# Two-layer decoder trunk: transposes of the norm dealt over two banks by pairs of blocks, bias table in 32 copies, no adaLN steps in the value part

## The chip, the cores and the metric

One NeuronCore of a Trainium2 chip runs the whole kernel as one program. The metric is device microseconds of one execution. The chip shares its work among TensorE (PE: matmuls and transposes; its weight loads are PEld), VectorE (DVE), ScalarE (ACT), GpSimd (POOL), SyncE (SP, which here only issues DMAs) and 16 DMA engines.

## What is computed

```python
for l in range(2):                                   # x is 256 x 1024, float32
    mod = silu(c) @ w_ada[l] + b_ada[l]              # adaLN: 9 vectors of 1024
    h = pre(x, 0); x += 0.5 * mod[0, 2] * (silu(h @ wg) * (h @ wu)) @ wd        # FFN, d_ff 2816
    h = pre(x, 1)                                    # pre: rmsnorm(x) * gain * (1 + scale) + shift
    q, k, v, ..., gates = split(h @ w_in[l])         # 4 stick-breaking, 6 dilated, 6 sliding-window heads
    x += mod[1, 2] * (sum_b sigmoid(g_b) * (o_b @ w_br_b)) @ w_out
    h = pre(x, 2); x += 0.5 * mod[2, 2] * (silu(h @ wg2) * (h @ wu2)) @ wd2     # second FFN
return rmsnorm(x)
```

The dilated and sliding-window heads add a bias to their scores: for each head a row of 383 values by distance (-1e30 where a key is masked), of which query row p takes the 256 values from 127 - p on.

## The kernel before

**Numbers.** Every weight and every activation is split in two fp32r parts, a high part H (a cast) and a low part L (the remainder), and each product is three matmuls: H by H, H by L, L by H. All weights, 280 MB, are read from HBM once.

**Units.** The weights come as 1 MB pieces (`raw`, three buffers) on SP's DMA queue, and each piece is cut in two units of 128 x 1024. `feed` (line 147) keeps five units ahead of PE: ACT casts a unit's high part (`wH`, line 144), DVE subtracts to get the low part (`wL`, line 160), and when a piece's last unit is subtracted, `load_raws` issues the load of the next piece. PE waits for a unit only when these run late. All instructions are issued in an order that is written out by hand; each engine and each queue runs its own list in order.

**Six sub-layers** (s = 0 to 5: FFN, mixer, FFN, FFN, mixer, FFN). The adaLN vectors of later sub-layers are computed in between: `ada_tick`, called once for every unit, adds to a credit by the table `PACE` (line 48; one tuple for each sub-layer, one number for each of its parts, scaled so that the steps due are done in time) and runs `ada_step` for each whole credit: a 512 KB load on SP's queue and a multiply-add of 128 x 1024 on DVE (L284; the first of each eight on ACT, L282). For the mixers (s = 1 and 4) the parts are: the six units of the value part, the 14 of q and k, the three gated branches (10, 10 and 12), and the output.

**The change of sub-layers** (`run_rows`, line 765). The 256 tokens are two halves, t = 0 and 1. While PE ends the last matmuls of half 1, the norm of half 0 runs: `norm_x` scales x (`xn`), `norm_pe` (line 484) has PE transpose its eight blocks of 128 features into two PSUM banks (`psn`), blocks 0 to 3 in the first and 4 to 7 in the second, and `norm_evac` (line 495) applies scale and shift on the way out: DVE takes the first bank (L508), ACT the second (L510), four blocks each, into `h32`. `norm_high` (line 520, L523) casts one half of the features on ACT to the high part of the new `hHL`, `norm_low` (line 525, L529) subtracts on DVE. Between the casts ACT still squares the last quarter of x for half 1 (`jk`, line 455). Then PE runs `early()`: the first two units of the next sub-layer for half 0 (`ffn_early` line 852, `v_early` line 1009), which read these features; for an FFN both units read blocks 0 to 3, for a mixer unit 0 reads blocks 0 to 3 and unit 1 blocks 4 to 7. After them comes the same for half 1, where the high part is written straight from PSUM.

**Bias table.** In the first FFN `bias_table` (line 426) adds the mask on DVE (`mk`, 12 heads x 383) and writes it eight times over to a DRAM tile `scr` with eight DMAs on POOL's queue (L433). At the start of each mixer `load_bias` (line 435) loads the 128 x 12 x 256 table `Tm` with 16 DMAs on POOL's queue (L442), each for eight neighbouring partitions; partition r + i takes its rows from copy i, shifted by one value. The table is first used in the dilated branch, some 75 us later.

**Stick-breaking heads.** Among the q and k units of a mixer run, for two pairs of heads (`sb_stages`, placed by line 1245): scores `pz`, exponentials on ACT (`e`, L1045), sums by PE (`pc`, L1057), a subtraction on DVE (`z`, L1060), the exponential of it on ACT (L1064), and PE's product with v (`po`, L1073).

Of the kernel before, what the change touches and what calls it, by code (L numbers as in the profile page):

```python
# [10 lines left out]
F32 = mybir.dt.float32  # L11
# [5 lines left out]
P = 128  # L17
# [3 lines left out]
KB = D // P  # L21
FF = 2816
NF = FF // P
NHEAD = 12
NDIST = 383
# [19 lines left out]
N1 = (0, 0, 1, 1, 0, 0)  # L45

START_PACE = 0.3
PACE = ((1, 0.75, 1, 1.25), (1, 1, 1, 1, 0.75, 0.75), (1, 1, 1, 1), (1, 1, 1, 0.75), (1, 2, 0, 0, 1, 2),
        (1, 1, 1, 1))
SPARE = (5, 1, 1, 1, 1, 1)  # L50
SOON = 5
# [38 lines left out]
class Trunk:  # L90
# [335 lines left out]
    def bias_table(self):  # L426
        nc, oh, mk, rb = self.nc, self.oh, self.mk, self.rb
        p = self.ps("psr")
        nc.tensor.matmul(p[:NHEAD, :NDIST], rb, oh, start=True, stop=True)
        nc.vector.tensor_tensor(mk, p[:NHEAD, :NDIST], mk, op=ALU.add)  # L430
        self.scr = self.dp.tile([NHEAD, 8, NDIST], F32, tag="scr", name="scr")
        for r in range(8):
            nc.gpsimd.dma_start(self.scr[:, r, :], mk)  # L433

    def load_bias(self, T):


        for r in range(0, P, 8):
            base = self.scr[:, 0:8, 0:256]
            src = bass.AP(tensor=base.tensor, offset=base.offset + P - 1 - r,  # L440
                          ap=[[NDIST - 1, 8], [8 * NDIST, NHEAD], [1, 256]])
            self.nc.gpsimd.dma_start(T[r:r + 8], src)  # L442


    def square(self, t, cols, tag):
# [37 lines left out]

    def norm_pe(self, t, s, xn):

        ps = []
        for q in range(2):
            p = self.ps(f"psn{s}_{t}_{q}")
            for i in range(4):
                fb = 4 * q + i  # L490
                self.nc.tensor.transpose(p[:, i * P:(i + 1) * P], xn[:, fb * P:(fb + 1) * P], self.ident)
            ps.append(p)
        return ps

    def norm_evac(self, t, s, ps, between=()):

        nc = self.nc
        h32 = self.work([P, KB, P], f"h32_{s}_{t}")
        sl = slice(t * P, (t + 1) * P)

        def evac(out):
            for i in range(4):
                for q in range(2):
                    fb = 4 * q + i
                    sa, sb = self.modv[:, s, 1, fb:fb + 1], self.modv[:, s, 0, fb:fb + 1]
                    src = ps[q][:, i * P:(i + 1) * P]
                    if q == 0:
                        nc.vector.tensor_scalar(out[:, fb, :], src, sa, sb, ALU.mult, ALU.add)  # L508
                    else:
                        nc.scalar.activation(out[:, fb, :], src, AF.Identity, bias=sb, scale=sa)  # L510

        if t == 1:
            evac(self.hH[:, :, sl])
            for f in between:
                f()
            self.feed(2)
        evac(h32)
        return h32

    def norm_high(self, t, h32, q):  # L520
# [244 lines left out]
    def run_rows(self, us, s, xh, xl, early=None):  # L765
# [54 lines left out]
        piece(1, end, tail[LEAD:])  # L820
        self.done(TAIL)
        h0 = self.norm_evac(0, s + 1, p0)
        self.norm_high(0, h0, 0)
        self.mean_eps(1)
        self.residual(1, end, s, pd[1, end])
        self.norm_high(0, h0, 1)
# [1 line left out]
        left = [(ch[1], self.ada_reduce(ch)) for ch in nxt[:n1]]  # L828
# [5 lines left out]
        p1 = self.norm_pe(1, s + 1, xn1)  # L834
        left += [(ch[1], self.ada_reduce(ch)) for ch in nxt[n1:]]
        for kind, fs in left:
            if kind < 2:
                fs[0]()
        h1 = self.norm_evac(1, s + 1, p1, [fs[1] for kind, fs in left if kind < 2])
        self.norm_low(1, h1)  # L840
        self.feed()
        for kind, fs in left:
            if kind == 2:
# [7 lines left out]

    def ffn_early(self, plan):

        for u in plan["in"][:2]:
            u.pe(u, (0,))

    def run_ffn(self, plan, early=None):
        s = plan["s"]
# [150 lines left out]
    def v_early(self, plan):  # L1009

        s = plan["s"]
        plan["pv"] = [[self.ps(f"pv{s}_{t}_{i}") for i in range(2)] for t in range(2)]
        for i, part in enumerate(("all", "high")):
            self.v_pe(i, plan["v"][i], plan["pv"], (0,), part)

    def v_post(self, t, pv):
# [252 lines left out]
    def run(self):  # L1269
# [100 lines left out]
        for n, plan in enumerate(plans):  # L1370
# [7 lines left out]
            else:  # L1378
                k = len(plan["in"])
                parts = [k // 4, k // 4, k - k // 4 * 2, NF - TAIL]  # L1380
            self.pace = sum(([w] * k for w, k in zip(PACE[s], parts)), [])
            f = need / sum(self.pace)
# [42 lines left out]
```

## Time and profile before

| | |
|---|---|
| three executions | 1200.52, 1202.75, 1202.95 us; median 1202.75 |
| the profiled execution | 1201.48 us, its span 1199.7 us, mean granted clock 0.995 |
| PE (matmul) busy | 1172.9 us, 98% of the span, 7105 instructions |
| weight loads, DVE, ACT, POOL busy | 1023.3, 830.7, 607.4, 37.8 us |
| DMA | 285.15 MB, 238 GB/s in the mean; SP's queue 279.88 MB, POOL's queue 3.93 MB |
| chain that ended last | PE 84%, DMA 5%, DVE 4%, ACT 4% |

PE is nearly always busy, so a change is worth what it takes from PE's idle time, of which there are 27 us in all, or from the time in which PE runs at a lower clock. The start of the program and its end hold most of the idle time; the rest is a few waits of about 1 us.

### The profile page before, as it was taken

Reading aid. Unit: us, or ns where it says so; the run is one execution under the profiler, and the core shown is the slowest. Engines: PE = TensorE matmul, PEld = TensorE weight load, DVE = VectorE, ACT = ScalarE, POOL = GpSimd, SP = SyncE. Lnnn points to the kernel's source line nnn. Section 1 sums busy time; section 2 is a strip of 40 time slices with the busy share of each in tenths; the row PEclk is TensorE's granted clock in tenths of the full one; section 3 lists DMA queues with packets and bytes.
Section 4 is the critical chain, followed back from the end, with each engine's and each line's share of the span. In section 5 each row is a group of like instructions: output and inputs, shape, how many; then the busy total and the mean of one; then the engine's idle time right before and its main releaser. Section 6 shows DMA issues by size and latency. Waiting matters only on the chain.

```text
span 1199.7 us, 17743 instructions
## 1 busy us (share of the span) xinstructions
PE 1172.9 (98%) x7105; PEld 1023.3 (85%) x7105; DVE 830.7 (69%) x1011; ACT 607.4 (51%) x877; POOL 37.8 (3%) x74
## 2 busy tenths in 40 slices
PE   6999999999999999999999999999999999999997
PEld 6988888989999878888878888889999997888886
DVE  3677777667788787677677676665866787555544
ACT  5554443565564465444365444355655446544432
POOL 1001000300000000000000000011000000000000
PEclk9999999999999999999999999999999999999999
DMA  9988889796568668888839877759863573665550
GB/s 319 310 317 308 282 300 332 120 339 210 195 200 308 228 231 295 282 299 277 287 121 335 280 252 270 251 162 210 283 208 110 185 268 139 223 196 182 182 176 36
DMA packets 151516, 285.15 MB, mean 238 GB/s; under 512 B 8006, under 2 KB 78956, under 8 KB 151432
## 3 DMA queue, kind: packets, MB, share of 16 engines
q1 hardware_dynamic: 148744, 279.88, 68.9%
q0 software_dynamic: 2544, 3.93, 2.5%
q8 instruction: 56, 0.92, 0.3%
q14 instruction: 28, 0.23, 0.1%
q10 hardware_dynamic: 144, 0.20, 0.0%
HBM read 282.77 MB, written 1.20 MB: 237 GB/s over the span
## 4 chain that ended last, share of the span: by engine, by line
PE 84%; DMA 5%; DVE 4%; ACT 4%; issue 2%; POOL 1%; SPq 0%; POOLq 0%; ACTq 0%; DVEq 0%
PE pf L672 35%; PE pd L763 21%; PE pg L603 12%; PE pq L603 4%; PE pb L603 3%; DMA raw<-in_w_in 2%; PE pf L633 2%; PE pft L698 2%; DVE wL L160 1%; DMA ada<-in_w_ada 1%; PE adag L345 1%; ACT wH L144 1%; ACT jk L455 1%; DVE acc L284 1%; ACT h L510 1%
## 5 line engine op out<-in xcount | busy, mean ns | idle before, releaser
L160 DVE TENSOR_TENSOR wL<-raw,wH 128x1024 fp32r<-128x1024 f32 (+1 forms) x384 | 462.2, 1212 | 264.5 <-ACT wH L144 262.2
L144 ACT CAST wH<-raw 128x1024 fp32r<-128x1024 f32 (+1 forms) x384 | 395.8, 1045 | 386.7 <-PE pf L672 155.1
L672 PE MATMUL pf<-wH,hHL 128*128 128x512 f32 (+1 forms) x1408 | 418.5, 378 | 3.4 <-ACT hHL L523 3.4
L672 PEld LDWEIGHTS pf<-wH,hHL 128*128 128x128 f32 x1408 | 258.6, 188 | 53.8 <-ACT hHL L523 4.3
L672 PE MATMUL pf<-wL,hHL 128*128 128x512 f32 (+1 forms) x704 | 260.9, 375 | 0.0
L672 PEld LDWEIGHTS pf<-wL,hHL 128*128 128x128 f32 x704 | 132.6, 188 | 23.7 <-issue 0.7
L284 DVE SCALAR_TENSOR_TENSOR acc<-ada,sc,acc 128x1024 f32<-128x1024 f32 x112 | 143.3, 1279 | 3.9 <-DMA ada<-in_w_ada 3.9
L603 PE MATMUL pg<-hHL,wH 128*128 128x256 f32 x768 | 145.4, 285 | 0.0
L763 PE MATMUL pd<-wH,ffH 128*128 128x512 f32 x336 | 131.6, 392 | 0.0
L763 PE MATMUL pd<-wH,ffL 128*128 128x512 f32 x336 | 130.8, 389 | 0.0
L763 PE MATMUL pd<-wL,ffH 128*128 128x512 f32 x336 | 130.8, 389 | 0.0
L603 PEld LDWEIGHTS pg<-hHL,wH 128*128 128x128 f32 x768 | 121.8, 192 | 2.7 <-issue 0.9
L603 PE MATMUL pg<-hHL,wL 128*128 128x256 f32 x384 | 94.0, 283 | 0.0
L603 PE MATMUL pq<-hHL,wH 128*128 128x256 f32 x448 | 85.4, 289 | 1.0 <-ACT wH L144 1.0
L763 PEld LDWEIGHTS pd<-wH,ffH 128*128 128x128 f32 x336 | 63.1, 188 | 13.6 <-issue 0.8
L763 PEld LDWEIGHTS pd<-wH,ffL 128*128 128x128 f32 x336 | 63.1, 188 | 13.3
L763 PEld LDWEIGHTS pd<-wL,ffH 128*128 128x128 f32 x336 | 63.1, 188 | 12.8
L603 PEld LDWEIGHTS pq<-hHL,wH 128*128 128x128 f32 x448 | 71.8, 195 | 2.0 <-ACT wH L144 1.2
L603 PEld LDWEIGHTS pg<-hHL,wL 128*128 128x128 f32 x384 | 73.4, 191 | 0.0
L603 PE MATMUL pq<-hHL,wL 128*128 128x256 f32 x224 | 56.1, 287 | 1.8 <-DVE wL L160 1.8
L603 PEld LDWEIGHTS pq<-hHL,wL 128*128 128x128 f32 x224 | 43.6, 195 | 2.4 <-DVE wL L160 2.1
L702 ACT CAST ffH<-pft 128x512 fp32r<-128x512 f32 (+1 forms) x44 | 22.4, 560 | 45.2 <-PE pft L698 45.2
(210 smaller groups left out, 1200.4 us busy)
## 6 DMA issues: line engine op xcount, KB each, us to landing
ada<-in_w_ada SPq DMA_DIRECT2D x128, 512.0 KB, 5.4
raw<-in_w_ffn_down SPq DMA_DIRECT2D x44, 1024.0 KB, 5.1
raw<-in_w_in SPq DMA_DIRECT2D x42, 1024.0 KB, 6.7
raw<-in_w_ffn_gate SPq DMA_DIRECT2D x41, 1024.0 KB, 6.2
raw<-in_w_ffn_up SPq DMA_DIRECT2D x41, 1024.0 KB, 5.2
first<-in_w_ada SPq DMA_DIRECT2D x32, 256.0 KB, 6.0
raw<-in_w_out SPq DMA_DIRECT2D x8, 1024.0 KB, 7.1
raw<-in_w_ffn_gate SPq DMA_DIRECT2D x12, 256.0 KB, 6.0
```

The lines of the kernel that those rows point to most:

```text
L144: self.nc.scalar.copy(u.H, u.view(self.raw_tiles[u.raw]))
L160: nc.vector.tensor_tensor(u.L, u.view(self.raw_tiles[u.raw]), u.H, op=ALU.subtract)
L284: self.nc.vector.scalar_tensor_tensor(acc, src, sc, acc, ALU.mult, ALU.add)
L345: nc.tensor.matmul(ps[h], self.ones, acc[:, h * 512:(h + 1) * 512], start=True, stop=True)
L455: nc.scalar.activation(junk[:, :w], self.x[:, t, lo:lo + w], AF.Square, scale=1.0 / 32.0, accum_out=ms[:, n:n + 1])
L510: nc.scalar.activation(out[:, fb, :], src, AF.Identity, bias=sb, scale=sa)
L603: nc.tensor.matmul(out, w[:, kb, cs], x[:, kb, :], start=i == 0, stop=i == n - 1)
L633: self.nc.tensor.matmul(ps[fb][:, S * up:S * up + S], w[:, 2 * k + up, b * P:(b + 1) * P], x[:, 2 * q + k, :], start=q == 0 and not up and ...
L672: self.nc.tensor.matmul(out, x[:, k0 + k, sl], w[:, k, :], start=k0 == 0 and i == 0, stop=k0 + nk == KB and i == 3 * nk - 1)
L698: nc.tensor.transpose(pt[:, i * P:(i + 1) * P], f[:, t, i * P:(i + 1) * P], self.ident)
L702: nc.scalar.copy(H, src)
L763: self.nc.tensor.matmul(out, x[:, kb, sl], w[:, 0, hs], start=first and i == 0, stop=last and i == 2)
```

## The change

Lines of the changed kernel stand some 5 later than those of the kernel before from `norm_evac` on (L508 is L507, L510 L509, L523 L529, L529 L535, L672 L678, L284 unchanged).

- **Banks.** `norm_pe` still transposes blocks 0 to 7 in order, but blocks 0, 1, 4, 5 now lie in the first bank and 2, 3, 6, 7 in the second. `norm_evac` goes by halves of the features, DVE with two blocks and ACT with two in each. For t = 0 the cast of the first half's high part stands between the two halves. For t = 1 the subtraction of each half follows that half.
- **Early units.** `ffn_early` runs the H parts of both units before their L parts. `v_early` is written in another way, but its order is the same.
- **Bias table.** 32 copies, written by one DMA; four loads of 32 partitions each, every fourth partition.
- **PACE.** For both mixers the value part has 0, and the other parts share what is due.

```diff
-PACE = ((1, 0.75, 1, 1.25), (1, 1, 1, 1, 0.75, 0.75), (1, 1, 1, 1), (1, 1, 1, 0.75), (1, 2, 0, 0, 1, 2),
+PACE = ((1, 0.75, 1, 1.25), (0, 1.25, 1, 1, 0.75, 0.75), (1, 1, 1, 1), (1, 1, 1, 0.75), (0, 1.5, 0.5, 0.5, 1, 1),
...
-        self.scr = self.dp.tile([NHEAD, 8, NDIST], F32, tag="scr", name="scr")
-        for r in range(8):
-            nc.gpsimd.dma_start(self.scr[:, r, :], mk)
+        self.scr = self.dp.tile([NHEAD, 32, NDIST], F32, tag="scr", name="scr")
+        nc.gpsimd.dma_start(self.scr, mk.unsqueeze(1).to_broadcast([NHEAD, 32, NDIST]))
...
-        for r in range(0, P, 8):
-            base = self.scr[:, 0:8, 0:256]
+        for r in range(4):
+            base = self.scr[:, 0:32, 0:256]
             src = bass.AP(tensor=base.tensor, offset=base.offset + P - 1 - r,
-                          ap=[[NDIST - 1, 8], [8 * NDIST, NHEAD], [1, 256]])
-            self.nc.gpsimd.dma_start(T[r:r + 8], src)
+                          ap=[[NDIST - 4, 32], [32 * NDIST, NHEAD], [1, 256]])
+            self.nc.gpsimd.dma_start(T[r::4], src)
...
+        ps = [self.ps(f"psn{s}_{t}_{q}") for q in range(2)]
+        for fb in range(KB):
+            self.nc.tensor.transpose(self.norm_block(ps, fb), xn[:, fb * P:(fb + 1) * P], self.ident)
         return ps
+
+    def norm_block(self, ps, fb):
+        i = fb % 2 + fb // 4 * 2
+        return ps[fb // 2 % 2][:, i * P:(i + 1) * P]
...
-        evac(h32)
+            for half in range(2):
+                evac(h32, half)
+                self.norm_low(1, h32, (half,))
+        else:
+            evac(h32, 0)
+            self.norm_high(0, h32, 0)
+            evac(h32, 1)
...
-        for u in plan["in"][:2]:
-            u.pe(u, (0,))
+        for part in ("high", "low"):
+            for u in plan["in"][:2]:
+                u.pe(u, (0,), part)
...
-        for i, part in enumerate(("all", "high")):
+        for i, part in ((0, "high"), (0, "low"), (1, "high")):
```

What moves on the engines is shown at three places. The first is ACT's list at the change from the first mixer to the second FFN, before and after (`h` is h32, `jk` a square, `psn_0` and `psn_1` the transposes of half 0 and half 1; numbers at the end of names count tiles):

```order
L455 ACTIVATE jk_11_4194,ms_1_4176<-x 128x256
L510 ACTIVATE h_2_0_4219<-psn_0_1_4205,modv 128x128 x4
L523 CAST hHL_4196<-h_2_0_4219 128x4x128
L455 ACTIVATE jk_12_4233,ms_1_4176<-x 128x256
L523 CAST hHL_4196<-h_2_0_4219 128x4x128
L481 ACTIVATE xn_1_4253<-x,r_1_4250 128x512
```

```order
L454 ACTIVATE jk_11_4175,ms_1_4157<-x 128x256
L509 ACTIVATE h_2_0_4200<-psn_0_1_4182,modv 128x128 x2
L529 CAST hHL_4177<-h_2_0_4200 128x4x128
L509 ACTIVATE h_2_0_4200<-psn_0_1_4182,modv 128x128 x2
L454 ACTIVATE jk_12_4214,ms_1_4157<-x 128x256
L529 CAST hHL_4177<-h_2_0_4200 128x4x128
```

The first cast of hHL stands after two of the four evacuations, where it stood after all four; what follows it is as before, behind two more evacuations.

The second is PE's list right after that, the first units of the second FFN for half 0 (`pf`; the first unit's wH and wL are 4092 and 4094 before, 4073 and 4075 after; the second's 4110 and 4112, 4091 and 4093):

```order
L672 MATMUL pf_0_0_0_4237<-wL_4094,hHL_4196 128x512
L672 MATMUL pf_0_0_0_4237<-wH_4092,hHL_4196 128x512 x2
L672 MATMUL pf_0_0_0_4237<-wH_4110,hHL_4196 128x512
L672 MATMUL pf_0_0_0_4237<-wL_4112,hHL_4196 128x512
L672 MATMUL pf_0_0_0_4237<-wH_4110,hHL_4196 128x512
L672 MATMUL pf_0_0_0_4237<-wL_4112,hHL_4196 128x512
L672 MATMUL pf_0_0_0_4237<-wH_4110,hHL_4196 128x512 x2
```

```order
L678 MATMUL pf_0_0_0_4218<-wL_4075,hHL_4177 128x512
L678 MATMUL pf_0_0_0_4218<-wH_4091,hHL_4177 128x512
L678 MATMUL pf_0_0_0_4218<-wL_4093,hHL_4177 128x512
L678 MATMUL pf_0_0_0_4218<-wH_4091,hHL_4177 128x512
L678 MATMUL pf_0_0_0_4218<-wL_4093,hHL_4177 128x512
L678 MATMUL pf_0_0_0_4218<-wH_4073,hHL_4177 128x512 x2
L678 MATMUL pf_0_0_0_4218<-wH_4091,hHL_4177 128x512 x2
```

The two matmuls with the low part of hHL (the rows with x2) stood behind each unit's own four and now stand behind all eight.

The third is DVE's list in the value part of the first mixer, from its first adaLN step on, and after the change up to its first step, which comes later in the program:

```order
L284 SCALAR_TENSOR_TENSOR acc_2_1754<-ada_1842,sc,acc_2_1754 128x1024
L160 TENSOR_TENSOR wL_2157<-raw_1885,wH_2155 128x1024
L160 TENSOR_TENSOR wL_2165<-raw_1885,wH_2163 128x1024
L160 TENSOR_TENSOR wL_2175<-raw_2078,wH_2173 128x1024
L284 SCALAR_TENSOR_TENSOR acc_2_1754<-ada_1865,sc,acc_2_1754 128x1024
L160 TENSOR_TENSOR wL_2206<-raw_2078,wH_2204 128x1024
```

```order
L160 TENSOR_TENSOR wL_2153<-raw_2071,wH_2151 128x1024
L160 TENSOR_TENSOR wL_2181<-raw_2071,wH_2179 128x1024
L160 TENSOR_TENSOR wL_2211<-raw_2079,wH_2209 128x1024
L160 TENSOR_TENSOR wL_2243<-raw_2079,wH_2241 128x1024
L160 TENSOR_TENSOR wL_2274<-raw_2145,wH_2272 128x1024
L284 SCALAR_TENSOR_TENSOR acc_2_1747<-ada_1835,sc,acc_2_1747 128x1024
```

The adaLN steps (L284) between the subtractions are gone; the subtractions of the value part follow each other, and the first step stands behind that of the first q and k piece's successor, wL_2274. In numbers of steps, by the table: first mixer value part 3 to 0, q and k 7 to 9, second branch 5 to 6; second mixer value part 1 to 0, q and k 9 to 7, first two branches 0 to 2 each, output 3 to 2. The 512 KB loads move along SP's queue with their steps.

## Rows read from the trace of the kernel before

**Rows 1.** Waits of PE: line, releaser, us in total, times, longest.

```profile
PE pf L672 <- ACT hHL L523: 3.4, 3, 1.3
PE pv L1006 <- ACT hHL L523: 2.1, 2, 1.3
PE pq L603 <- DVE wL L160: 1.8, 2, 0.9
PE po L1073 <- ACT z L1064: 1.1, 1, 1.1
PE pq L603 <- ACT wH L144: 1.0, 1, 1.0
```

**Rows 2.** Timeline of ACT, change to the second FFN: start, us, instruction, [idle before].

```profile
418.13 1.49 ACT L510 ACTIVATE h<-psn,modv 128x128 f32<-128x128 f32 x4
419.50 0.62 ACT L523 CAST hHL<-h 128x512 fp32r<-128x512 f32 x1
420.01 0.43 ACT L455 ACTIVATE jk<-x 128x256 bf16<-128x256 f32 x1
...
421.64 0.72 ACT L481 ACTIVATE xn<-x,r 128x512 f32<-128x512 f32 x1 [0.60 <-POOL r L470]
```

**Rows 3.** Timeline of PE and of DVE (last row) at the same place.

```profile
418.57 0.28 PE L763 MATMUL pe<-wH,mHL 128*128 128x256 f32 x1
420.18 0.50 PE L672 MATMUL pf<-wH,hHL 128*128 128x512 f32 x1 [1.33 <-ACT hHL L523]
...
423.08 1.03 PE L491 MATMUL psn<-ident,xn 128*128 128x128 f32 x8
...
419.35 0.42 DVE L540 TENSOR_TENSOR x<-x,y 128x256 f32<-128x256 f32 x1
```

**Rows 4.** Windows, first mixer: busy us of each engine, granted clock, DMA share, GB/s.

```profile
228.00:233.00 5.00, 5.00 (x44) 5.00 (x43) 5.00 (x6) 2.28 (x3) 2.95 (x6) 1.00 1.07 99
...
243.20:246.03 2.83, 0.97 (x7) 0.65 (x6) 1.74 (x2) 1.99 (x2) 0.00 (x0) 1.00 1.09 359
246.03:249.95 3.92, 3.92 (x23) 3.92 (x22) 3.92 (x4) 3.39 (x6) 0.00 (x0) 0.56 1.08 364
249.95:270.00 20.05, 20.05 (x158) 18.50 (x157) 14.20 (x17) 14.58 (x18) 0.00 (x0) 1.00 1.06 364
```

**Rows 5.** DMA queues in 220 to 246 us: packets, MB, share of 16 engines; issues; POOL's timeline.

```profile
q0 software_dynamic: 1024, 1.58, 54.8%
q1 hardware_dynamic: 2145, 2.36, 40.9%
...
Tm<-scr POOLq DMA_DIRECT2D x16, 96.0 KB, 6.7
...
221.20 5.88 POOL L442 DMA_DIRECT2D Tm<-scr  x10 [0.69 <-issue]
```

**Rows 6.** Chain of waits, first mixer and (after the dots) second mixer: start, us.

```profile
228.47 14.64 DMA raw<-in_w_in
...
815.50 14.13 DMA raw<-in_w_in
...
838.68 7.08 DMA ada<-in_w_ada
```

**Rows 7.** Timelines, stick-breaking heads: second mixer's PE, then first mixer's ACT and PE.

```profile
866.31 0.87 PE L1073 MATMUL po<-z,qkv 128*64 128x256 f32 x8 [1.06 <-ACT z L1064]
...
279.05 0.85 ACT L1064 ACTIVATE z<-z 128x768 f32<-128x768 f32 x1 [0.79 <-DVE z L1060]
...
281.44 0.87 PE L1073 MATMUL po<-z,qkv 128*64 128x256 f32 x8
```

**Rows 8.** Timeline of POOL at the table's copies; waits from 90 to 213 us; the page's group L284.

```profile
111.10 4.07 POOL L433 DMA_DIRECT2D scr<-mk  x8 [101.95 <-DVE mk L430]
...
ACT wH L144 <- PE pf L672: 27.3, 16, 3.4
...
L284 DVE SCALAR_TENSOR_TENSOR acc<-ada,sc,acc 128x1024 f32<-128x1024 f32 x112 | 143.3, 1279 | 3.9 <-DMA ada<-in_w_ada 3.9
```

More of the change, by code (lines that the diff above doesn't have):

```diff
@@ L484, in norm_pe @@
     def norm_pe(self, t, s, xn):
[L486 to L492, printed above, removed]
-        return ps
+        ps = [self.ps(f"psn{s}_{t}_{q}") for q in range(2)]
+        for fb in range(KB):
+            self.nc.tensor.transpose(self.norm_block(ps, fb), xn[:, fb * P:(fb + 1) * P], self.ident)
+        return ps
+    def norm_block(self, ps, fb):
+        i = fb % 2 + fb // 4 * 2
+        return ps[fb // 2 % 2][:, i * P:(i + 1) * P]
     def norm_evac(self, t, s, ps, between=()):
@@ L499, in norm_evac, with evac @@
         sl = slice(t * P, (t + 1) * P)
-        def evac(out):
-            for i in range(4):
+        def evac(out, half):
+            for i in range(2):
                 for q in range(2):
-                    fb = 4 * q + i
+                    fb = 4 * half + 2 * q + i
                     sa, sb = self.modv[:, s, 1, fb:fb + 1], self.modv[:, s, 0, fb:fb + 1]
-                    src = ps[q][:, i * P:(i + 1) * P]
+                    src = self.norm_block(ps, fb)
                     if q == 0:
@@ L512, in norm_evac @@
         if t == 1:
-            evac(self.hH[:, :, sl])
+            for half in range(2):
+                evac(self.hH[:, :, sl], half)
             for f in between:
@@ L516, in norm_evac @@
             self.feed(2)
-        evac(h32)
+            for half in range(2):
+                evac(h32, half)
[4 more added lines that the diff above has]
+            evac(h32, 1)
         return h32
@@ L822, in run_rows @@
         h0 = self.norm_evac(0, s + 1, p0)
-        self.norm_high(0, h0, 0)
         self.mean_eps(1)
@@ L838, in run_rows @@
                 fs[0]()
-        h1 = self.norm_evac(1, s + 1, p1, [fs[1] for kind, fs in left if kind < 2])
-        self.norm_low(1, h1)
+        self.norm_evac(1, s + 1, p1, [fs[1] for kind, fs in left if kind < 2])
         self.feed()
```

## The prediction

> **What bounds the kernel now.** PE is busy for 1172.9 of the 1199.7 us of the span, so the first view is the list of what PE waited for [rows 1]. Outside the program's start two things stand there. Five times PE waits for a cast of hHL (pf three times, 3.4 us in all; pv twice, 2.1): that is each change of sub-layers. And the mixers' first q and k units wait for weights, 1.8 us on wL and 1.0 on wH, and po waits 1.1 for ACT. The second view is the timeline of such a change [rows 2, 3]: ACT's four evacuations, the cast, and PE, which had ended its last matmul at 418.85 and starts 0.06 us after the cast. The third is the chain of waits through a mixer [rows 6]: behind the wait for weights stands a 1 MB load that takes 14.64 us, in the second mixer one of 14.13. The fourth, the windows and the DMA queues of that stretch [rows 4, 5], says why: the DMA engines are full (share 1.07), yet move 99 GB/s. POOL's queue, the bias table, holds 54.8% of the 16 engines for 1.58 MB; SP's queue moves 2.36 MB in 40.9%.
>
> The sum is made against the profiled execution, 1201.48 us, of which 1.78 lie outside the span.
>
> **A. Banks and the earlier cast.** ACT's four evacuations last 1.49 us, and the cast begins 1.37 after the first [rows 2], so one takes 0.34 to issue and the last 0.47 to end. Now the cast comes after two: it reads ACT's own second block too, so it can start at 418.13 + 0.34 + 0.47 = 418.94, say 418.97, where it started at 419.50: **0.53 us** earlier. DVE's two blocks start later, because the first bank is now full after the sixth transpose, not the fourth; eight last 1.03 [rows 3], so 0.2 to 0.3 later, and they still end before ACT's. Each of the five waits is longer than that (the 2.1 us of pv are 1.3 and 0.8 [rows 1]), so PE starts 0.53 earlier.
>
> What is late next: the square jk. It followed the cast by 0.51 [rows 2]; now two evacuations come between, 418.97 + 0.51 + 2 x 0.34 = 420.16 against 420.01, so about 0.16 later, and with it the chain to xn of half 1 (421.64 + 0.16 + 0.72 = 422.5). PE would reach the transposes of half 1 at 423.08 - 0.53 = 422.55: no wait. In a mixer unit 1 needs the second cast, also 0.16 late, so PE loses about 0.14 of its gain there. The subtraction for the L parts needs the cast and x, ready at 419.77 [rows 3], so it starts where the cast ends. PE asks for it eight matmuls after its start: 12 take 2.90 us in an FFN [rows 3], so 1.9 later, since both H parts run first; in a mixer, with half the columns, 1.0. That is what the new order of the early units is for, and alone it costs and gives nothing. Half 1's evacuation has the same instructions; no wait of PE stands on it in the list, so nothing. The early value units keep their order: nothing. Sum: 3 x 0.53 + 2 x 0.39 = **-2.4**. Bounds: 0 (ACT's last square sets the end anyway) and the whole idle time, 5.5.
>
> **B. Bias table, first mixer.** [...] That costs (1 - 0.56) x 3.92 = 1.72 more. Together 3.6. What does the new table load take? It moves the same 1.58 MB in the same rows of 256 values. Lower bound of its rate: as now, 99 GB/s; upper bound: that of weights in this stretch, 359 to 364 [rows 4]. By [rows 5] a packet of the table (1.5 KB) holds an engine for 0.548 x 16 x 26 / 1024 = 0.22 us, one of SP's queue (1.1 KB) for 0.079. So the slowness belongs to the table's loads, not to small packets, and what sets them apart is eight neighbouring partitions at a time and a source of eight copies; both go. I take a rate near the weights': 1.58 MB issued from 221.2 on [rows 5] are in by about 229, and the load of 228.47, 2.9 us of data, lands by 236. Needed it is about 240.3: PE runs dry at 243.2, 0.4 earlier by A, and cast and subtraction took some 2.5 us from the landing. So **-3.6**; bounds -3.6 and, with rival 4, +3.1.
>
> [...]
>
> Removing the adaLN steps from the value part takes 512 KB loads and 1.28 us of DVE each [rows 8] out of this stretch. On SP's queue they stood behind the load of 228.47, so alone they cannot bring that one earlier: nothing by itself. POOL's queue gets four issues for 16, and its next work is the norm at the mixer's end: nothing. The 32 copies write 0.59 MB for 0.15. Cover: at that place ACT waits for PE, 27.3 us over the stretch [rows 8], so weights are ahead; the eight copies took 4.07 us, 32 at that rate 16. Nothing; if that cover were gone, 2 or 3 us.
>
> **C. Second mixer.** The same load (14.13 us) leaves one gap, the other 0.9 of wL; the chain goes on through an adaLN load of 7.08 and DVE's list to po, which waits 1.06 [rows 1, 6, 7]. The 0.9 goes with the table's load. Of the 1.06 I take half, since steps still stand between (seven where nine stood). Sum **-1.4**; bounds -2.0 and 0.
>
> **D. Steps moved to q and k.** The first mixer gets nine steps there for seven, 1.28 us of DVE each [rows 8]. One more ahead of z's subtraction makes z that much later. Slack: ACT's exponential of z ends at 279.90, po starts at 281.44 [rows 7], so 1.54. That just holds. I add **+0.3**; bounds 0 and +2.8 (a wait as in the second mixer now, 1.06, and one fall of the clock, 1.72).
>
> Sum: -2.4 - 3.6 - 1.4 + 0.3 = -7.1, so 1194.4 for an execution like the profiled one. The median of the three runs is 1.27 above it and would give 1195.6. I take the middle, **1195.0 us**; from the middle before, 1202.1, the rivals are reckoned too.
>
> **Rivals.**
> 1. *The banks give nothing* (the change doesn't do what it says: the first half is out no earlier). DVE's blocks now wait for six transposes, and the cast for both engines. Against: ACT, not DVE, ended last. Then +2.4: 1197.4. Chance 0.08.
> 2. *The table's load is no faster, and the wait stays.* Then only A is left: 1202.1 - 2.4 = 1199.7. For: all loads read the same small DRAM tile. Against: the packets above. Chance 0.10.
> 3. *The wait moves to the stick-breaking heads of the first mixer*, for 1.06 and a fall of the clock: 1195.0 + 2.8 - 0.3 = 1197.5. For: the second mixer with nine steps shows it. Against: there DVE was late from the start of the stretch. Chance 0.14.
> 4. *Slower: 32 copies take longer to read than eight.* The table holds all 16 engines for 0.548 x 26 = 14.2 us now, 0.22 a packet. At half as much again, 0.33, issued at once from 222 on and ahead of the weights, it would end at 243.3 and the next 1 MB at 246.2, 3.1 us later than now: +3.1 in each mixer, and a fall of the clock in the second too, 1.72. That is 7.9 - 2.4 = +5.5, about 1207.6. It decides from 0.24 us a packet on (a table that ends after 237.4). For: the source grows to four times its size, and nothing in the trace says that the partitions are to blame rather than the source. Against: the source then has a copy for every partition of a load, as before. Chance 0.06.
>
> **How the numbers follow.** My forecast has 0.60; 0.02 is left for the unnamed. About 0.2% (2.4 us) is what a measurement of this kernel can tell from no change: faster means under 1200.3. The forecast and rivals 1 and 3 are faster, 0.82, and half of rival 2: 0.87. Same: the other half and the unnamed, 0.07. Slower: rival 4, 0.06. The range: down to 1191.0, A with all 5.5 us and C with 2.0 (3.7 less); up to 1199.5, which takes in rivals 1, 3 and half of 2. Outside are rival 4, the rest of rival 2 and the ends: under 0.2.
>
> **What would show it.** Right: the waits of PE for hHL fall from 5.5 us to about 3; pq's waits on wL and wH are gone; the clock stays at 1.00 around 246; in the stretch from 221 DMA moves over 250 GB/s; the load that took 14.64 us takes under 8. A is wrong if ACT's cast starts less than 0.4 earlier against its first evacuation. B is wrong if the DMA share is full at about 100 GB/s again. D shows as a new wait of po in the first mixer. The whole is wrong if a wait of over 1 us appears at a place that the list does not have now.

## The result and the profile after

| | median us | executions |
|---|---|---|
| before, beside the change | 1201.76 | 1200.52 to 1202.95 (4) |
| after | 1194.41 | 1194.18 to 1194.67 (4) |

The ratio is 0.9939, with a 95% interval of 0.9922 to 0.9956: faster by 0.6%, three times what a measurement of this kernel can tell from no change. The profiled execution of after took 1194.19 us, 7.29 less than the profiled one of before. The forecast was 1195.0.

The waits of PE first, outside the program's start; the columns are those of [rows 1]. Of the five lines there three are gone (both of pq, and po), two are half as long, and one is new:

```profile
PE pf L678 <- ACT hHL L529: 1.7, 3, 0.8
PE pv L1011 <- ACT hHL L529: 1.0, 2, 0.8
PE pt_swa L1178 <- DVE p_swa L1166: 0.9, 1, 0.9
```

The same change of sub-layers as in [rows 2, 3], timelines of ACT and then of PE:

```profile
415.31 0.79 ACT L509 ACTIVATE h<-psn,modv 128x128 f32<-128x128 f32 x2
416.13 0.62 ACT L529 CAST hHL<-h 128x512 fp32r<-128x512 f32 x1
416.66 0.80 ACT L509 ACTIVATE h<-psn,modv 128x128 f32<-128x128 f32 x2
...
416.80 0.50 PE L678 MATMUL pf<-wH,hHL 128*128 128x512 f32 x1 [0.77 <-ACT hHL L529]
```

The cast now begins 0.82 us after the first evacuation, where it began 1.37 after it, and PE's gap is 0.77 where it was 1.33.

The first mixer in windows (columns as in [rows 4]), then its DMA queues from 220 to 246 us:

```profile
228.00:233.00 5.00, 5.00 (x43) 5.00 (x42) 5.00 (x5) 2.09 (x3) 0.00 (x0) 1.00 0.59 201
...
243.00:246.00 3.00, 3.00 (x28) 3.00 (x27) 3.00 (x4) 1.53 (x2) 0.00 (x0) 1.00 0.49 148
246.00:250.00 4.00, 4.00 (x36) 4.00 (x35) 3.09 (x3) 1.89 (x2) 0.00 (x0) 1.00 0.98 336
```

```profile
q1 hardware_dynamic: 4575, 4.62, 54.8%
q0 software_dynamic: 448, 1.57, 18.6%
...
Tm<-scr POOLq DMA_DIRECT2D x4, 384.0 KB, 5.0
```

The same table, which held 54.8% of the engines' time [rows 5], holds 18.6%, and SP's queue moved twice as much in the same stretch. PE has no gap from 243 to 246 us, and its clock stays at 1.00 behind it. The weight load that took 14.64 us [rows 6] is issued at 228.80, and its cast starts at 234.09, so it is in within 5.3 us:

```profile
234.09 2.00 ACT L144 CAST wH<-raw 128x1024 fp32r<-128x1024 f32 x2 [4.00 <-DMA raw<-in_w_in]
```

The new wait stands in the sliding-window heads of the first mixer, 69 us behind po. DVE's timeline, then PE's:

```profile
343.65 1.28 DVE L284 SCALAR_TENSOR_TENSOR acc<-ada,sc,acc 128x1024 f32<-128x1024 f32 x1
344.84 0.16 DVE L1161 TENSOR_TENSOR sm_swa<-sm_swa 128x6 f32<-128x6 f32 x1
...
345.26 1.43 DVE L1166 TENSOR_TENSOR p_swa<-p_swa,sm_swa 128x768 f32<-128x768 f32 x2
...
346.84 1.18 PE L1178 MATMUL pt_swa<-ident,p_swa 128*128 128x128 f32 x9 [0.89 <-DVE p_swa L1166]
```

An adaLN step (L284) stands right ahead of the softmax's last operations, on which PE's transposes wait. It is one of the steps that the new PACE put elsewhere; in before a subtraction of weights stands there, and DVE is idle ahead of it:

```profile
345.21 1.22 DVE L160 TENSOR_TENSOR wL<-raw,wH 128x1024 fp32r<-128x1024 f32 x1 [1.53 <-ACT wH L144]
346.35 0.16 DVE L1156 TENSOR_TENSOR sm_swa<-sm_swa 128x6 f32<-128x6 f32 x1
```

The account by the waits: hHL -2.8, pq -2.8, po and pc -1.2, clock -1.7 (window 246 to 250), pt_swa +0.9, and +0.4 at the program's start: -7.2 of the 7.29 measured.

### The profile page after: what moved, and what is told of

Read it like the earlier page. It is cut to its first block, busy times and chain, and to the rows that moved or that the text cites. A ratio compares the mean times of both kernels' runs of the same rounds, so it can differ in the third digit from the quotient of the medians.

```text
span 1192.5 us, 17699 instructions
## 1 busy us (share of the span) xinstructions
PE 1171.1 (98%) x7105; PEld 1021.8 (86%) x7105; DVE 830.5 (70%) x1011; ACT 608.1 (51%) x877; POOL 20.9 (2%) x43
## 4 chain that ended last, share of the span: by engine, by line
PE 90%; DVE 3%; ACT 2%; DMA 2%; issue 2%; POOL 1%; SPq 0%; POOLq 0%; ACTq 0%; DVEq 0%
PE pf L678 36%; PE pd L769 21%; PE pg L609 11%; PE pq L609 7%; PE pv L1011 3%; PE pf L639 3%; PE pb L609 3%; PE pft L704 2%; PE adag L345 1%; ACT jk L454 1%; DVE wL L160 1%; DMA first<-in_w_ada 1%; DMA raw<-in_w_in 1%; DMA raw<-in_w_ffn_gate 1%; DMA ada<-in_w_ada 0%
## 5 line engine op out<-in xcount | busy, mean ns | idle before, releaser
L678 PE MATMUL pf<-wH,hHL 128*128 128x512 f32 (+1 forms) x1408 | 418.5, 378 | 1.7 <-ACT hHL L529 1.7
L678 PEld LDWEIGHTS pf<-wH,hHL 128*128 128x128 f32 x1408 | 258.6, 188 | 52.1 <-ACT hHL L529 2.6
L678 PE MATMUL pf<-wL,hHL 128*128 128x512 f32 (+1 forms) x704 | 261.0, 375 | 0.0
L678 PEld LDWEIGHTS pf<-wL,hHL 128*128 128x128 f32 x704 | 132.6, 188 | 23.9 <-issue 0.7
L284 DVE SCALAR_TENSOR_TENSOR acc<-ada,sc,acc 128x1024 f32<-128x1024 f32 x112 | 143.3, 1279 | 4.9 <-DMA ada<-in_w_ada 4.9
L609 PEld LDWEIGHTS pq<-hHL,wL 128*128 128x128 f32 x224 | 42.9, 191 | 0.2 <-issue 0.2
```

What stands on the lines that cost most here:

```text
L284: self.nc.vector.scalar_tensor_tensor(acc, src, sc, acc, ALU.mult, ALU.add)
L609: nc.tensor.matmul(out, w[:, kb, cs], x[:, kb, :], start=i == 0, stop=i == n - 1)
L678: self.nc.tensor.matmul(out, x[:, k0 + k, sl], w[:, k, :], start=k0 == 0 and i == 0, stop=k0 + nk == KB and i == 3 * nk - 1)
```

## The experiments

The theory: the table's load is slow because of the partitions that the loads under way write at one time; this alone starves the weights (B and C). The banks give 0.5 us at each change (A). The steps' new places give nothing (D). Rivals: the copies or the number of loads make the table slow; the steps in the value part starved the weights; the parts need each other.

All ratios below are to the kernel before, run on the same chip beside each group of experiments; its medians were 1202.31 (e1 to e4), 1201.10 (e5 to e8), 1202.75 (e10, e13, e15) and 1202.43 (e16). The second and the last group ran on other chips than the rest, and after's chip is not on record, so tenths of a us between groups say little. All its executions lay between 1198.78 and 1204.49.

### Each part alone

**e1, the table alone** (before, with the change's `bias_table` and `load_bias`).

```diff
-        self.scr = self.dp.tile([NHEAD, 8, NDIST], F32, tag="scr", name="scr")
-        for r in range(8):
-            nc.gpsimd.dma_start(self.scr[:, r, :], mk)
+        self.scr = self.dp.tile([NHEAD, 32, NDIST], F32, tag="scr", name="scr")
+        nc.gpsimd.dma_start(self.scr, mk.unsqueeze(1).to_broadcast([NHEAD, 32, NDIST]))
...
-                          ap=[[NDIST - 1, 8], [8 * NDIST, NHEAD], [1, 256]])
-            self.nc.gpsimd.dma_start(T[r:r + 8], src)
+                          ap=[[NDIST - 4, 32], [32 * NDIST, NHEAD], [1, 256]])
+            self.nc.gpsimd.dma_start(T[r::4], src)
```

> The bias table alone, as 32 copies in four loads of every fourth partition; banks and adaLN steps as in the kernel before. My theory (B and C are the table's doing alone): the weight load that took 14.64 us is in within 8 us, PE's waits of 1.8 on wL and 1.0 on wH are gone, and the clock stays at 1.00 around 246 us: -2.8 - 1.7 = -4.5 us, and -1.1 more if po's wait in the second mixer goes with it: 1196.2 to 1197.3 us against a median of 1201.8. The five waits for hHL stay at 5.5 us. Rival (the adaLN steps taken out of the value part were what freed the weights): the waits on wL and wH stay for the most part and the time is within 1.5 us of before. Rival (the parts need each other): less than 3 us faster.

Measured: **1195.12 us** (1194.48 to 1195.52), 0.9944 [0.9930, 0.9957]. The waits for hHL stand at 5.5 us as before, and all others of [rows 1] are gone, pq and po, and with them 0.2 us on pc (the sums of the stick-breaking heads) that stood further down the list. It is more than the theory's 4.5 to 5.6. Where it comes from is seen in the times at which PE starts the norm's transposes ahead of a mixer (psn) and the first po in it; PE's timeline of e1, first and second mixer, then the two of before that are not in [rows 7]:

```profile
214.97 1.26 PE L490 MATMUL psn<-ident,xn 128*128 128x128 f32 x8
277.11 0.87 PE L1072 MATMUL po<-z,qkv 128*64 128x256 f32 x8
...
796.91 1.26 PE L490 MATMUL psn<-ident,xn 128*128 128x128 f32 x8
859.20 0.87 PE L1072 MATMUL po<-z,qkv 128*64 128x256 f32 x8
```

```profile
215.41 1.27 PE L491 MATMUL psn<-ident,xn 128*128 128x128 f32 x8
...
801.16 1.26 PE L491 MATMUL psn<-ident,xn 128*128 128x128 f32 x8
```

From psn to po the first mixer takes 62.14 us where before took 281.44 - 215.41 = 66.03, so -3.9. The second takes 62.29 where before took 866.31 - 801.16 = 65.15, so -2.9. The rival that the steps were what held up the weights falls: they are where they were.

**e2, banks, early cast and early units alone** (after, with the old table and the old PACE).

```diff
-PACE = (..., (0, 1.25, 1, 1, 0.75, 0.75), ..., (0, 1.5, 0.5, 0.5, 1, 1), ...)
+PACE = (..., (1, 1, 1, 1, 0.75, 0.75), ..., (1, 2, 0, 0, 1, 2), ...)
...
-        for r in range(4):
+        for r in range(0, P, 8):
...
-            self.nc.gpsimd.dma_start(T[r::4], src)
+            self.nc.gpsimd.dma_start(T[r:r + 8], src)
```

> The banks, the earlier cast and the early units' order alone; bias table and adaLN steps as in the kernel before. My theory (A): PE's waits for hHL fall from 5.5 us to about 2.7, the other waits stay: -2.4 to -2.8 us, 1199.0 to 1199.4 us. Two changes of five lead into a mixer; there the first pq waits for weights, so up to 1.1 us of it may be given back at that wait: then 1199.5 to 1200.4. Rival (the banks give nothing without the table): 1201.0 or more.

Measured: 1198.80 us (1197.12 to 1201.41), 0.9973 [0.9962, 0.9983]. The waits for hHL are 2.7 us, as expected, and part of the gain is given back where the theory looked for it, at the first pq of the mixers, 3.9 us where [rows 1] have 2.8:

```profile
PE pq L610 <- ACT wH L144: 2.2, 2, 1.9
PE pq L610 <- DVE wL L160: 1.7, 2, 0.9
```

By the waits this should be a gain of some 2 us, and it measured 3.5. This kernel's twelve executions, like those of before, are spread, the fastest at a mean granted clock of 0.998 (1197.12 us), the slowest at 0.994 (1201.41). So the 3.5 is no clean size for A.

**e3, the steps' new places alone** (before, with the change's PACE).

```diff
-PACE = (..., (1, 1, 1, 1, 0.75, 0.75), ..., (1, 2, 0, 0, 1, 2), ...)
+PACE = (..., (0, 1.25, 1, 1, 0.75, 0.75), ..., (0, 1.5, 0.5, 0.5, 1, 1), ...)
```

> The new places of the adaLN steps alone; banks and table as in the kernel before. My theory (nothing by itself): within 1.2 us of before, 1200.6 to 1203.0, the load at 228.5 us still takes 14 us or more, because those steps' loads stood behind it. The wait of 0.9 us of the first mixer's pt_swa for p_swa, which is new after the change, comes from this part and may show here. Rival (the steps in the value part kept the weights waiting, by their DMA and their share of DVE): 2 to 4 us faster, and PE's waits on wL and wH fall below 1 us together.

Measured: 1205.09 us (1203.28 to 1206.91), 1.0025 [1.0015, 1.0035]: slower, so the theory and its rival both missed the time. Two parts of the theory came true: the weights are as late as before (the load is issued at 228.54, and ACT has nothing to do from 233 to 243 us; in before its cast starts at 243.21), and the wait of pt_swa is there. In the second mixer the waits on po and pc are gone. In the first, three new ones came; the waits of PE from the page:

```profile
PE po L1073 <- ACT z L1064: 2.3, 1, 2.3
...
PE pc L1057 <- DVE e L1051: 1.1, 1, 1.1
PE pt_swa L1173 <- DVE p_swa L1161: 0.9, 1, 0.9
```

DVE's timeline there shows the cause of the longest: a step (L284) and an adaLN gate (L350) right ahead of the subtraction of z, which came at 282.03, with po at 283.97. Of e3 and then of before, where neither stands there:

```profile
279.64 1.28 DVE L350 TENSOR_TENSOR gate<-adag,gate 128x512 f32<-128x512 f32 x2
280.84 1.27 DVE L284 SCALAR_TENSOR_TENSOR acc<-ada,sc,acc 128x1024 f32<-128x1024 f32 x1
282.03 1.01 DVE L1060 TENSOR_TENSOR z<-z,pc 128x384 f32<-128x384 f32 x2
```

```profile
276.86 1.23 DVE L160 TENSOR_TENSOR wL<-raw,wH 128x1024 fp32r<-128x1024 f32 x1 [1.27 <-ACT wH L144]
278.00 1.01 DVE L1060 TENSOR_TENSOR z<-z,pc 128x384 f32<-128x384 f32 x2
```

**e16, table and new steps, without the banks** (e1 with e3's edit).

> Table and adaLN steps of the change, banks as in the kernel before. The runs so far give the table alone 1195.1 us, table and banks 1193.0, all three parts 1194.4. My theory (with the fast table the new places of the steps only cost, by the wait of pt_swa in the first mixer, whatever the banks are): that wait shows again with 0.8 to 1 us, and the time is 0.9 to 1.5 over the table alone: 1196.0 to 1196.6. Rival (the cost comes from the steps together with the earlier start that the banks give): 1195.5 or less and no such wait.

Measured: 1196.25 us (1195.47 to 1196.58), 0.9948 [0.9935, 0.9962]. The wait of pt_swa is there with 0.9 us; po and pc have none. Against e1 (on another chip) the steps' new places cost 1.1 us without the banks.

### What makes the table's load slow

Four kernels change only the table of before: **e4** the same eight copies and sixteen loads of eight partitions, but every sixteenth partition; **e5** 32 copies, sixteen loads of eight neighbours; **e6** 32 copies, four loads of 32 neighbours; **e15** is e4 with the sixteen loads in another order. The core of the edits, against before, and for e15 against e4:

```diff
 e4
-                          ap=[[NDIST - 1, 8], [8 * NDIST, NHEAD], [1, 256]])
-            self.nc.gpsimd.dma_start(T[r:r + 8], src)
+                          ap=[[NDIST - 16, 8], [8 * NDIST, NHEAD], [1, 256]])
+            self.nc.gpsimd.dma_start(T[r::16], src)
 e5
-            src = bass.AP(tensor=base.tensor, offset=base.offset + P - 1 - r,
+            src = bass.AP(tensor=base.tensor, offset=base.offset + P - 1 - r + (r // 8) % 4 * 8 * NDIST,
 e6
-        for r in range(0, P, 8):
+        for r in range(0, P, 32):
...
-            self.nc.gpsimd.dma_start(T[r:r + 8], src)
+            self.nc.gpsimd.dma_start(T[r:r + 32], src)
 e15
-        for r in range(16):
+        for k in range(16):
+            r = k % 4 * 4 + k // 4
```

> The kernel before with the same eight copies and the same sixteen loads, and only the partitions of a load changed: every sixteenth of 128 instead of eight neighbours. My theory (eight neighbouring partitions are what makes the table's load slow): the table comes in at more than 200 GB/s with the weights, the wait on weights goes as in the whole change, 1196.2 to 1197.5 us. Rival (the number of copies in DRAM, eight readers on one small tile): as before, 1201 to 1203, and the load at 228.5 us takes 14 us again. Rival (the number of loads, sixteen issues): as before too.

> The kernel before with 32 copies of the bias table in DRAM written by one DMA, but still sixteen loads of eight neighbouring partitions, spread over the copies. My theory (the partitions): as before, 1201 to 1203 us, the DMA engines full at about 100 GB/s in the stretch from 221 us. Rival (the source: eight copies in 147 KB are read from few places): the waits on weights go, 1196 to 1198 us.

> The kernel before with 32 copies and four loads, but of 32 neighbouring partitions each instead of every fourth one. My theory (how many ways into the SBUF a load reaches): two loads at a time run, so half to all of 128 partitions are reached; between before and the change, nearer to the change, 1196.5 to 1199 us. [...] Rival (only the every-fourth pattern helps): 1201 to 1203. Rival (number of loads alone): as the change, 1196 to 1197.

> The sixteen loads of every sixteenth partition again, with only their order changed: 0, 4, 8, 12, 1, 5, ... instead of 0, 1, 2, 3, .... In that earlier run such a load, though its eight partitions lie far apart, moved no more than 122 to 129 GB/s; 32 neighbours moved about 200, every fourth of 128 over 300. My theory (what counts is how many separate groups of partitions the loads under way at one time write, and loads whose first partitions are 0 and 1 write the same groups, those of 0 and 4 others): the stretch from 225 to 228 us moves 180 GB/s or more, and q0's share from 219 to 246 us falls from 42.9% to 25-32%. Rival (the size of a load: sixteen loads of 96 KB are slow in any order): 120 to 130 GB/s and a share of 40% or more. The time tells nothing between them: weights are in time in both, 1194.5 to 1196 us. [...]

In this table the last column is the share of the 16 engines' time that POOL's queue (q0), which here carries only the table, held.

| | median us | ratio | what the table's loads write | GB/s, 225 to 228 us | q0, 219 to 246 us |
|---|---|---|---|---|---|
| before | | 1 | 16 x 8 neighbours | 103 | 52.8% |
| e5 | 1199.41 | 0.9987 [0.9977, 0.9998] | 16 x 8 neighbours | 102 | 51.3% |
| e4 | 1195.13 | 0.9944 [0.9931, 0.9958] | 16 x every sixteenth, 0, 1, 2, ... | 122 | 42.9% |
| e15 | 1194.92 | 0.9938 [0.9924, 0.9952] | 16 x every sixteenth, 0, 4, 8, ... | 166 | 24.4% |
| e6 | 1195.33 | 0.9950 [0.9931, 0.9968] | 4 x 32 neighbours | 202 | 28.5% |
| after | 1194.41 | 0.9939 [0.9922, 0.9956] | 4 x every fourth | 240 | 17.9% |

The windows from which the table is read: in these 3 us only the table is loaded, and the last two columns are the DMA share and GB/s. Of before, e5, e4, e15, e6 and after, one fence each; after has a second row, because most of its table is in by 227 us:

```profile
225.00:228.00 3.00, 3.00 (x27) 3.00 (x26) 2.96 (x7) 3.00 (x5) 2.63 (x5) 1.00 1.08 103
```

```profile
225.00:228.00 3.00, 3.00 (x28) 3.00 (x27) 2.96 (x6) 3.00 (x5) 2.40 (x5) 1.00 1.07 102
```

```profile
225.00:228.00 3.00, 3.00 (x27) 3.00 (x27) 2.97 (x8) 3.00 (x7) 3.00 (x6) 1.00 1.05 122
```

```profile
225.00:228.00 3.00, 3.00 (x27) 3.00 (x26) 2.97 (x7) 3.00 (x8) 3.00 (x6) 1.00 0.63 166
```

```profile
225.00:228.00 3.00, 3.00 (x28) 3.00 (x27) 2.96 (x7) 3.00 (x6) 0.00 (x0) 1.00 1.05 202
```

```profile
225.00:228.00 3.00, 3.00 (x26) 2.95 (x25) 2.79 (x7) 3.00 (x5) 0.00 (x0) 1.00 0.66 240
224.00:227.00 3.00, 3.00 (x28) 3.00 (x27) 2.79 (x7) 3.00 (x6) 0.00 (x0) 1.00 0.99 335
```

The copies are cleared by e5 as the cause of the low rate: four times as many sources, the same rate. Its time lies below the 1201 to 1203 that I expected, and its interval ends just under 1: the cast of the late weights starts at 242.43, 0.8 us earlier than in before, and PE waits 2.0 us on pq where [rows 1] have 2.8. So the copies may be worth about 1 us of time, for which no reason is shown. The size of a load is cleared by e15: with the same sixteen loads the engines are busy for 0.63 in place of 1.05, q0's share falls from 42.9% to 24.4%, and a load lands in 3.1 us (median of the issues) where e4's took 5.6. Its 166 GB/s, below the 180 that I expected, is no longer the engines' limit but the issue's: POOL needs 9.27 us for the sixteen,

```profile
222.44 9.27 POOL L443 DMA_DIRECT2D Tm<-scr  x16 [0.60 <-issue]
```

so 0.58 for 96 KB, 170 GB/s. What is left is which partitions the loads under way write at one time. With the engines full (share 0.99 to 1.08) eight neighbours to a load move 102 and 103 GB/s, 32 neighbours 202, every fourth partition 335 (224 to 227 us): neighbours hold each other up. They do so also across two loads: e4's order (0 and 1 next to each other) moves 122 at a share of 1.05, nearly as slow as eight neighbours, and e15's 166 at 0.63. That was my error in e4: the partitions of one load are not enough, those of the next count too.

Why partitions that lie near each other hold each other up is not shown by any run here, nor are the ways into the SBUF (the memory that the table is loaded into) of which e6's theory speaks: they are an assumption of mine, and what e6 shows is the 202 GB/s.

That the loads land in twos is taken from before, where POOL issues its last six loads in twos at 227.46, 229.39 and 231.32 us, each pair when earlier loads have landed: 192 KB in 1.93 us, 102 GB/s. That two and no more are written at a time, as e6's theory has it, is my estimate from these times.

The times say nothing of this: e4, at 122 GB/s, is as fast as e6 at 202 and as e1. The table only has to be out of the way early enough: in e4 the cast of the late weights starts at 241.18, only 2.0 us earlier than in before, and PE waits for no weights. A time alone would have called e4 a proof of the wrong reason.

### What the rest is worth

**e10, after with the adaLN steps at their old places** (e3's edit undone). **e13** is e10 with e8's edit.

> The kernel after with the adaLN steps at their old places. My theory (the steps' new places buy nothing, and cost the wait of 0.9 us of the first mixer's pt_swa): that wait is gone and none comes in its place, -0.9 us against the kernel after: 1193.2 to 1193.8. Rival (without them po waits in the second mixer again, as before the change): a wait of po of 0.5 to 1.1 us there, 1194 to 1195. Rival (the new places are needed for the weights): pq waits again, 1196 or more.

> The kernel after with both: adaLN steps at their old places and the square of half 1's second piece behind the first cast. My theory (the two act in different stretches and add): -0.9 and -0.6 against the kernel after's 1194.4, 1192.6 to 1193.2 us, with PE's waits for hHL at 1.5 us and none on pt_swa, pq or po. Rival (an earlier PE runs into the next thing that is late): 1193.3 to 1194, with a new wait of over 0.4 us in a mixer.

Measured: e10 **1192.98 us** (1192.23 to 1193.12), 0.9918 [0.9904, 0.9932]; e13 **1192.51 us** (1192.09 to 1192.81), 0.9917 [0.9903, 0.9930]. Neither has a wait on pt_swa, pq or po. Both are faster than the change, whose executions all lie above 1194.1. By the medians the steps' new places cost 1.4 us. Of this the traces show 1.0: from the first mixer's po to the next psn after takes 136.10 us, e10 135.07; PE's timelines, after and e10:

```profile
277.60 0.87 PE L1078 MATMUL po<-z,qkv 128*64 128x256 f32 x8
...
413.70 1.26 PE L487 MATMUL psn<-ident,xn 128*128 128x128 f32 x8
```

```profile
277.87 0.87 PE L1078 MATMUL po<-z,qkv 128*64 128x256 f32 x8
...
412.94 1.27 PE L487 MATMUL psn<-ident,xn 128*128 128x128 f32 x8
```

**e7, after with the early units in their old order.**

```diff
-        for part in ("high", "low"):
-            for u in plan["in"][:2]:
-                u.pe(u, (0,), part)
+        for u in plan["in"][:2]:
+            u.pe(u, (0,))
```

> The kernel after with the two early FFN units in their old order (H and L of one unit, then of the next). My theory: the L part of the first unit then needs the subtraction about 1.0 us after PE's start instead of 1.9; after the change PE starts at 416.80 us and the subtraction ends at 417.60, so it asks at about 417.7 and just has it: same as after within 0.6 us, 1194.2 to 1195.0. Rival (the new order is needed once the cast comes earlier): a new wait of PE on hHL from DVE three times, 0.3 to 0.5 us each, 1195.2 to 1196.

Measured: 1194.23 us (1193.86 to 1195.86), 0.9942 [0.9928, 0.9957], as after, and no new wait on hHL's low part at a change.

**e8, after with one square later.** Ahead of ACT's first evacuation stands the square of half 1's second piece.

```diff
         for c in cols[1][:-1]:
             piece(1, c, tail)
-            self.residual(1, c, s, pd[1, c])
+            if last or c != cols[1][-2]:
+                self.residual(1, c, s, pd[1, c])
+            else:
+                self.gated(1, c, s, pd[1, c])
...
-        h0 = self.norm_evac(0, s + 1, p0)
+        h0 = self.norm_evac(0, s + 1, p0, [lambda: self.square(1, cols[1][-2], s + 1)])
...
             self.norm_high(0, h32, 0)
+            for f in between:
+                f()
             evac(h32, 1)
```

> The kernel after with one ACT instruction moved: the square of half 1's second piece (0.42 us and 0.19 for its accumulator), which stands ahead of half 0's evacuations, is issued behind the first cast of hHL. My theory (ACT's queue is what the five remaining waits for hHL, 2.7 us, come from, and the evacuations start only when that square is out): the evacuation starts about 0.4 us earlier, PE's waits for hHL fall from 2.7 to 0.7 to 1.2 us, -1.5 to -2.0: 1192.4 to 1192.9 us. Rival (the transposes or DVE's blocks set the cast as well): under 0.5 us faster. Rival (half 1 comes late, a wait turns up at its cast): no faster, 1194 to 1195.

Measured: 1193.83 us (1193.67 to 1194.33), 0.9938 [0.9924, 0.9951], 0.6 below after: so nearer to the rival's size, and with executions that overlap those of after. The waits for hHL fell from 2.7 to 1.5 us in all, PE's gap at the change shown from 0.77 to 0.47, not by the square's whole 0.4:

```profile
416.88 0.50 PE L680 MATMUL pf<-wH,hHL 128*128 128x512 f32 x1 [0.47 <-ACT hHL L531]
```

ACT is free 0.13 us before it starts the evacuation there, at 415.37; PE's eight transposes end at 415.33, so it is most likely they that set it now. With e10's steps the same edit gave 0.5 (e13), again with executions that overlap.

## Why the prediction was right, and where it was not

The total, -7.1 against the profiled execution, came out at -7.29; two of its terms were off, in opposite directions, so that it came this close is partly luck.

| part | predicted | by runs with and without it |
|---|---|---|
| table (B and C) | -5.0 | -7.2 (before to e1) |
| banks and cast (A) | -2.4 | -2.1 (e1 to e10), -1.8 (e16 to after) |
| steps (D) | +0.3 | +1.4 (e10 to after), +1.1 (e1 to e16) |

The last column takes medians of different groups of runs, in part on different chips, whose kernels before lie up to 1.6 us apart.

- **A** holds by its own steps. The cast starts 0.82 us after the first evacuation (0.81 was worked out from 0.34 + 0.47), PE starts 0.56 earlier at the change shown (0.53), and with the fast table e10 gains 2.1 on e1. The early units' new order gives nothing by itself, as said (e7). ACT had more to give: its own queue ahead of the first evacuation (e8).
- **B** holds in its size: -3.9 between psn and po of the first mixer, 3.6 predicted. The 3.6 are 1.86 us in which PE stands, the gap of [rows 4], and 1.72 of clock. But the 1.72 is a fall of the clock (in before 0.50 from 246.5 to 249.5 us) that not every trace of a kernel with late weights has (last section). The rate near the weights' that I took for the new load was an estimate; after moved 335 GB/s from 224 to 227 us, where weights moved at 359 to 364 [rows 4]. The prediction named the partitions and the copies together; that it is the partitions is shown (e15, e6, with e5 for the copies). A load of every sixteenth partition is slow together with its next (e4, 122 GB/s), not by itself (e15, 166); whether one of eight neighbours is slow by itself no run shows. Of the list of what would show it, one number failed: the stretch from 221 to 228 us moved 225 GB/s, not over 250, because the table was in before the weights were asked for.
- **C** was mis-sized: -1.4 predicted, -2.9 measured (e1). The step that failed is "of the 1.06 I take half, since steps still stand between". The list of DVE ahead of po was late only because the weights had been; with them in time, nine steps in q and k leave no wait at all (e1). The 0.9 of wL, the 1.06 of po and 0.2 of pc make 2.2. The other 0.7 the list of waits doesn't show, but PE's timeline of before does: a gap costs more than its listed idle time. PE's matmuls overlap: the nine in the third row are busy for 1.24 us, yet the next one starts 1.08 after the first of them. At the gap of wL it starts 2.29 after, so 1.21 are lost where the list has 0.88. Counted in this way against e1, po loses 1.13 and pc 0.33, together 2.67; the other 0.2 is a slower start of the matmuls behind the gaps: behind that of wL the second starts 0.23 after the first, where the next ones start 0.11 to 0.13 apart, and behind that of pc the third starts 0.51 after the first, where it is 0.43 in e1.

```profile
829.80 1.41 PE L603 MATMUL pq<-hHL,wH 128*128 128x256 f32 x9
832.09 0.39 PE L603 MATMUL pq<-hHL,wL 128*128 128x256 f32 x1 [0.88 <-DVE wL L160]
...
833.99 1.24 PE L603 MATMUL pq<-hHL,wH 128*128 128x256 f32 x9
835.07 0.28 PE L603 MATMUL pq<-hHL,wL 128*128 128x256 f32 x1
```

- **D** had the wrong place and size. "One more ahead of z's subtraction makes z that much later" happens only with the slow table, as rival 3 has it: e3 shows po with 2.3 and pc with 1.1 in the first mixer. With the fast table po has none. I reckoned only with q and k, where PACE puts more steps, but a table that gives other shares moves every step behind it too, and one landed ahead of the sliding-window softmax. That wait, 0.9 us, is just under the 1 us that the prediction had set as the sign that the whole is wrong.
- **Rivals 1, 2 and 4** (banks, table no faster, table slower) fell with e2, e1 and the 17.9% of q0. No experiment made a table that is slower than before, and none left the table alone out of the change.
- **Removing the steps from the value part**, put at nothing by itself, holds for what it was said of, the weights: in e3 they are as late as before, and pq waits 2.6 us for 2.8. What makes e3 slower by 2.8 us is where the steps went, which is D.
- The lower end of the range is 3.7 below 1195.0, so 1191.3 and not 1191.0; nothing hangs on it.

## What to carry to other kernels

DMAs that write eight neighbouring partitions each filled the DMA engines at about 100 GB/s here (103 at a share of 1.08), where weights moved at 359 to 364, and what they held up was another queue's load (14.64 us, with the new table at most 5.3). Read the queue's share beside its MB, and change the partitions or only the order of the loads before the number or the source. When several parts of a change act on one stretch, run each alone and each left out: here the gain of the table hid the cost of the steps' new places, and leaving these out (e10) beats the change by some 1.0 to 1.4 us.

## What the runs showed that I had not expected

A gap of PE doesn't always bring the clock down. The window behind the first mixer's gap in e3, with PE idle for 2.13 of the 3 us before it, has 1.00; before has 0.56 in the mean behind 1.86 us of gap [rows 4].

```profile
243.00:246.00 3.00, 0.87 (x6) 0.47 (x5) 1.39 (x2) 1.99 (x2) 0.00 (x0) 1.00 1.09 345
246.00:250.00 4.00, 4.00 (x34) 4.00 (x35) 2.19 (x2) 3.36 (x6) 0.00 (x0) 1.00 1.06 331
```

Of the four profiled kernels with late weights, before and e2 (0.60 from 246 to 250 us) show the fall, e3 and e5 don't. So the 1.72 us of clock in term B seem to be paid in some executions and not in others; no kernel here has two traces that would show it. The times fit: 21 executions of before, at a mean clock of 0.994 to 0.999, spread over 5.7 us, those of e2, e3 and e5 over 3.6 to 4.3, while the five of e1, at 0.998 to 0.999, spread over 1.0. Without the wait the kernel was steadier as well as faster; that the clock is what makes the times spread is not shown.

The same shows in the program's start. From 18 to 20 us the clock is 0.50 in before and in after and 1.00 in e1 (windows, after and then e1):

```profile
18.00:20.00 2.00, 2.00 (x10) 2.00 (x11) 1.36 (x2) 2.00 (x5) 0.00 (x0) 0.50 1.09 347
```

```profile
18.00:20.00 2.00, 1.32 (x12) 1.12 (x10) 1.82 (x2) 2.00 (x5) 0.00 (x0) 1.00 1.10 350
```

It costs little there, because PE at full clock waits more: after reaches the first mixer's psn at 215.62 us, e1 at 214.97. But the mean clock of a run and PE's busy time (in the first 30 us 20.66 us in after, 19.50 in e1) differ by it, and neither was a sign of anything that the change does.
